# Two output projections of a two-layer decoder trunk, written as seven products of half blocks

## The chip, the core and the metric

The kernel runs on one core of one Trainium2 chip. TensorE (PE in the profile) multiplies matrices; VectorE (DVE), ScalarE (ACT) and GpSimd (POOL) work on the elements; SyncE (SP) issues nearly all the DMAs of the kernel before. Each engine works through its own list of instructions in order and waits where an operand isn't there yet. Operands lie in SBUF (128 partitions), and matmuls add into banks of PSUM. The metric is the device time of one execution in microseconds, as the median of several runs; it is smaller when the kernel is faster.

## What is computed

512 tokens of width 1024 pass through two layers and a last norm, all in float32. Each layer norms its input, projects it to many branches, makes an array of 2048 channels from them and projects that back to 1024 with a residual addition:

```python
def even_layer(x, norm_g, w_in, pool_w, pool_scale, ws, bs, w_out):
    h = rmsnorm(x, norm_g)
    z = h @ w_in
    ...
    return x + jnp.concatenate([y_a, y_b], axis=-1) @ w_out

def odd_layer(x, norm_g, w_in, conv_w, w_out):
    ...
    return x + jnp.concatenate([y_c, y_d], axis=-1) @ w_out

def reference(...):
    h = x
    for layer in range(DEPTH):      # DEPTH = 2: one even, one odd layer
        ...
    return rmsnorm(h, final_norm)
```

The change concerns the two products with `w_out` (512 x 2048 by 2048 x 1024), the additions into x behind them, and the norm that follows each.

## The kernel before

A product of two float32 arrays is made from three products of rounded parts. Each operand is split into a high part, rounded to the type of the matmul, and a low part, the rest; `mm3` adds high by high, high by low and low by high into one bank. The split of a weight tile (128 x 2048, 1 MB) is `weights`: SP loads it into `raw` (three buffers), ACT copies it to `hi` (L76), DVE subtracts to get `lo` (L77). `wh` and `wl` have two buffers each. The split of other arrays is `split` (L83 on ACT, L84 on DVE). Layer inputs are normed per tile of 128 tokens (`normed`: the addition into x on DVE, L99, squares with a sum on ACT, L100, a few tiny operations, two scalings on DVE, L110), then turned to channels on the partitions by PE and split again (`to_channels`: L119 on PE, L123 on ACT, L124 on DVE). The split layer input is `hth` and `htl`, two tiles that both layers use.

The array to be projected back is held as eight tiles `y[c]` of 256 channels by 512 tokens. The last operation on each half of them is a multiplication on Pool: L293 in the even layer (by the gate `sggb`, one operation for 256 channels), L489 and L519 in the odd layer. The Pool operation for the last tile runs while the projection has already begun.

`out_proj` does the projection in eight chunks c of 256 channels (`eo` after the even layer, `oo` after the odd one). A chunk loads and splits one weight tile (`eow`, `oow`) and splits `y[c]` (`eoy`, `ooy`); then for four token tiles t, two halves of the output h and two groups k of 128 channels it makes the three matmuls of `mm3`, 48 in a chunk and 384 in a projection, into eight banks. What ends it is a function given by the caller: `into_odd` takes chunks 6 and 7 token tile by token tile, norms each and begins to transpose tiles 0 and 1 between the matmuls; `finish` does the same for the final norm and stores the result. After the first projection the first product of the odd layer is `near` (bank and tile `v`, 96 matmuls in two groups c of two token tiles), which transposes tiles 2 and 3 before its second group; then comes `gates` (`gc`).

The order of work on each engine is the order in which the program writes it, apart from what waits for operands and for free buffers.

Of the kernel before, what the change touches and what calls it, by code (L numbers as in the profile page):

```python
# [9 lines left out]
F32 = mybir.dt.float32  # L10
# [20 lines left out]
def trunk(ctx, tc, x, w_even, w_eout, pool_w, ws_t, bs, par, g_even, w_odd, w_oout, g_odd, g_fin, cst, out):  # L31
# [19 lines left out]
    hth = cp.tile([P, KT, S], FR, name="hth")  # L51
    htl = cp.tile([P, KT, S], FR, name="htl")
    y = [cp.tile([P, 2, S], F32, name=f"y{c}") for c in range(8)]
# [8 lines left out]

    eps = cp.tile([P, 64], F32, name="eps")[:, 0:2]
# [4 lines left out]
    def weights(src, name, pieces=1):  # L68
        raw = wp.tile([P, CH], F32, tag="raw", name="r" + name, bufs=3)
# [3 lines left out]
        for i in range(pieces):  # L73
            at = slice(i * n, (i + 1) * n)
            nc.sync.dma_start(raw[:, at], src[:, at])
            A.activation(hi[:, at], raw[:, at], AF.Copy)  # L76
            V.tensor_sub(lo[:, at], raw[:, at], hi[:, at].bitcast(F32))  # L77
        return hi, lo

# [13 lines left out]
    def normed(tt, g, name, acc=None, then=None):  # L93
        o = sp.tile([P, D], F32, tag="xn", name=name, bufs=2)
# [20 lines left out]
    def to_channels(tt, o):  # L115
# [36 lines left out]
    def out_proj(src, name, last):  # L152
        acc = [[bank(f"{name}{t}{h}") for h in range(2)] for t in range(TT)]
        parts = {}

        def load(c):
            wh, wl = weights(src[c], f"{name}w{c}")
            parts[c] = (wh.rearrange("p (k d) -> p k d", k=2), wl.rearrange("p (k d) -> p k d", k=2),
                        *split(y[c], wp, "y", f"{name}y{c}"))

        def step(c, t, halves=(0, 1)):
            wh, wl, yh, yl = parts[c]
            tok = slice(t * P, (t + 1) * P)
            for h in halves:
                cols = slice(h * S, (h + 1) * S)
                for k in range(2):
                    mm3(acc[t][h], yh[:, k, tok], yl[:, k, tok], wh[:, k, cols], wl[:, k, cols],
                        c == 0 and k == 0, c == 7 and k == 1)
# [15 lines left out]
    with ExitStack() as ec:  # L184
# [6 lines left out]
        def v_half(c):  # L191
# [17 lines left out]
            if c == 0:  # L209
                load(0, 4)  # L210
                to_channels(0, normed(0, ge, "xa0"))
# [12 lines left out]
                for t in range(2):  # L224
                    step(t, 0)
                    step(t, 1)
                    to_channels(t + 1, o)
                    o = normed(t + 2, ge, f"xa{t + 2}")
                step(2, 0)
                to_channels(3, o)  # L230
# [50 lines left out]
        def mixer_b(g, vb):  # L281
# [9 lines left out]
            project(w_even[6 + 4 * g], f"u{g}", lambda j, acc: V.tensor_mul(mf[:, j, :], acc, mf[:, j, :]))  # L291
            sg = gate(w_even[7 + 4 * g], f"gb{g}")
            G.tensor_mul(mf, mf, sg)  # L293

# [9 lines left out]
    def into_odd(step, acc):  # L304
        def norm(t):
            o[t] = normed(t, go, f"xb{t}", acc[t])

        for t in range(2):
            step(6, t)
            step(7, t)  # L310
            norm(t)
        step(6, 2)
        to_channels(0, o[0])
        step(6, 3)
        step(7, 2)
        norm(2)
        to_channels(1, o[1])
        step(7, 3)
        norm(3)

    out_proj(w_eout, "eo", into_odd)
# [3 lines left out]
    with ExitStack() as oc:  # L325
# [3 lines left out]
        def values(p):  # L329
# [3 lines left out]
            def near():  # L333
# [168 lines left out]

        for c in range(4):
            dc, cv, zz = ([ap.tile([P, S + 2], F32, tag=f"qk{2 * i + j}", name=f"{n}{c}{j}", bufs=1) for j in range(2)]
# [24 lines left out]
    def finish(step, acc):  # L529
        for t in range(TT):  # L530
            for h in range(2):
                step(6, t, (h,))
                step(7, t, (h,))
# [86 lines left out]
```

## Time and profile before

| what | value |
|---|---|
| median of 3 runs | 1123.62 us (1123.47 to 1124.34) |
| the profiled execution | 1124.62 us |
| its span, first to last instruction | 1122.9 us |
| PE busy | 1105.0 us (98%) |
| DVE busy | 452.0 us (40%) |
| ACT busy | 357.5 us (32%) |
| POOL busy | 142.6 us (13%) |
| moved by DMA | 104.98 MB, mean 93 GB/s |
| first projection, first matmul to the next stage | 253.65 to 342.74 us |
| second projection, first matmul to the last addition | 1028.18 to 1115.65 us |

The profile is of one execution. Busy shares are averages over the whole span; what bounds a stretch is read from that stretch. Matmuls overlap in the records: the distance between two of them is the time that one costs, not the duration in its row.

### The profile page before, as it was taken

The page shows a single profiled execution, that of the slowest core. Times are in us where ns is not written, and L with a number is a line of the kernel's source. Part 1 is how long each engine was busy: PE and PEld are TensorE (multiplying, and loading weights), DVE is VectorE, ACT ScalarE, POOL GpSimd, SP SyncE. Part 2 cuts the span into 40 slices and gives each one's busy share as a digit, 9 for nine tenths or more (in the row PEclk, how much of TensorE's full clock was granted, in tenths as well). Part 3 has the DMA queues.
Part 4 walks back from the last instruction along what each step waited for, and adds up shares of the span by engine and source line. Part 5 has one row for each costly group of instructions (what it writes and reads, how often), then busy time and mean ns, then how long its engine had stood idle before and what let it go on. Part 6 is the DMA issues. An engine that isn't in the chain of part 4 may idle for free.

```text
span 1122.9 us, 12809 instructions
## 1 busy us (share of the span) xinstructions
PE 1105.0 (98%) x5288; PEld 945.4 (84%) x5288; DVE 452.0 (40%) x617; ACT 357.5 (32%) x532; POOL 142.6 (13%) x460
## 2 busy tenths in 40 slices
PE   6999999999999999999999999999999999999997
PEld 5888888888888988899889988899888888888885
DVE  6344315343256225433345225442445442432326
ACT  5323223222235224432424224332424222121323
POOL 0001000101000004320224004220124011011000
PEclk9999999999999999999999999999999999999999
DMA  9232232322323231222221221322221222323211
GB/s 331 88 118 85 75 112 85 109 79 75 113 75 111 96 113 45 106 75 75 100 90 62 89 93 57 105 84 76 81 108 44 107 90 99 113 76 113 76 38 75
DMA packets 18282, 104.98 MB, mean 93 GB/s; under 512 B 2096, under 2 KB 3248, under 8 KB 6704
## 3 DMA queue, kind: packets, MB, share of 16 engines
q1 hardware_dynamic: 18224, 104.17, 26.5%
q8 instruction: 41, 0.67, 0.2%
q14 instruction: 17, 0.14, 0.0%
HBM read 102.06 MB, written 2.10 MB: 93 GB/s over the span
## 4 chain that ended last, share of the span: by engine, by line
PE 98%; DMA 1%; ACT 0%; DVE 0%; SPq 0%; issue 0%; DVEq 0%
PE q L90 8%; PE q L88 8%; PE q L89 8%; PE v L88 6%; PE v L90 5%; PE v L89 5%; PE oo L88 3%; PE eo L90 3%; PE eo L88 3%; PE oo L90 3%; PE eo L89 3%; PE oo L89 3%; PE gc L88 1%; PE gc L89 1%; PE gc L90 1%; PE dx L90 1%
## 5 line engine op out<-in xcount | busy, mean ns | idle before, releaser
L88 PE MATMUL q<-hth,hq 128*128 128x512 f32 x384 | 150.5, 392 | 0.0
L90 PE MATMUL q<-hth,lq 128*128 128x512 f32 x384 | 149.6, 389 | 0.0
L89 PE MATMUL q<-htl,hq 128*128 128x512 f32 x384 | 149.5, 389 | 0.0
L88 PE MATMUL v<-hv,hth 128*128 128x512 f32 (+1 forms) x320 | 114.8, 359 | 0.9 <-ACT hth L123 0.9
L90 PE MATMUL v<-hv,htl 128*128 128x512 f32 (+1 forms) x320 | 112.8, 353 | 0.0
L89 PE MATMUL v<-lv,hth 128*128 128x512 f32 (+1 forms) x320 | 112.6, 352 | 0.0
L90 PEld LDWEIGHTS q<-hth,lq 128*128 128x128 f32 x384 | 72.1, 188 | 15.1
L89 PEld LDWEIGHTS q<-htl,hq 128*128 128x128 f32 x384 | 72.1, 188 | 14.6
L88 PEld LDWEIGHTS q<-hth,hq 128*128 128x128 f32 x384 | 72.2, 188 | 14.4
L88 PEld LDWEIGHTS v<-hv,hth 128*128 128x128 f32 x320 | 76.6, 239 | 4.7 <-ACT hth L123 2.1
L90 PEld LDWEIGHTS v<-hv,htl 128*128 128x128 f32 x320 | 76.5, 239 | 3.2 <-DVE htl L124 0.7
L89 PEld LDWEIGHTS v<-lv,hth 128*128 128x128 f32 x320 | 76.8, 240 | 2.7
L77 DVE TENSOR_TENSOR lq<-rq,hq 128x2048 fp32r<-128x2048 f32 x24 | 54.9, 2289 | 51.2 <-ACT hq L76 51.2
L76 ACT ACTIVATE hq<-rq 128x2048 fp32r<-128x2048 f32 x24 | 46.0, 1915 | 76.5 <-PE q L89 55.4
L77 DVE TENSOR_TENSOR lv<-rv,hv 128x2048 fp32r<-128x2048 f32 (+1 forms) x22 | 37.4, 1704 | 39.2 <-ACT hv L76 39.2
L90 PE MATMUL eo<-heow,leoy 128*128 128x512 f32 x128 | 49.9, 390 | 0.0
L89 PE MATMUL eo<-leow,heoy 128*128 128x512 f32 x128 | 49.8, 389 | 0.0
L88 PE MATMUL eo<-heow,heoy 128*128 128x512 f32 x128 | 49.8, 392 | 0.0
L89 PE MATMUL oo<-loow,hooy 128*128 128x512 f32 x128 | 49.7, 389 | 0.0
L90 PE MATMUL oo<-hoow,looy 128*128 128x512 f32 x128 | 49.7, 389 | 0.0
L88 PE MATMUL oo<-hoow,hooy 128*128 128x512 f32 x128 | 49.5, 390 | 0.0
L76 ACT ACTIVATE hv<-rv 128x2048 fp32r<-128x2048 f32 (+1 forms) x22 | 31.6, 1446 | 55.8 <-PE v L90 17.0
(218 smaller groups left out, 2167.7 us busy)
## 6 DMA issues: line engine op xcount, KB each, us to landing
rq<-in_w_odd SPq DMA_DIRECT2D x24, 1024.0 KB, 4.7
rv<-in_w_odd SPq DMA_DIRECT2D x12, 1024.0 KB, 4.7
reow<-in_w_eout SPq DMA_DIRECT2D x8, 1024.0 KB, 4.8
roow<-in_w_oout SPq DMA_DIRECT2D x8, 1024.0 KB, 4.7
ra<-in_w_even SPq DMA_DIRECT2D x4, 1024.0 KB, 4.7
rga<-in_w_even SPq DMA_DIRECT2D x4, 1024.0 KB, 5.5
ru<-in_w_even SPq DMA_DIRECT2D x4, 1024.0 KB, 4.8
rgb<-in_w_even SPq DMA_DIRECT2D x4, 1024.0 KB, 4.7
```

What stands on the lines that cost most here:

```text
L76: A.activation(hi[:, at], raw[:, at], AF.Copy)
L77: V.tensor_sub(lo[:, at], raw[:, at], hi[:, at].bitcast(F32))
L88: T.matmul(acc, ah, bh, start=first, stop=False)
L89: T.matmul(acc, ah, bl, start=False, stop=False)
L90: T.matmul(acc, al, bh, start=False, stop=last)
```

## The change

Both projections are done in Strassen's form. y is cut into 2 x 2 blocks (1024 channels by 256 tokens, `block[i, h]`, in one tile `yy`), w_out into four blocks of 1024 by 512, each stored as two tiles q of 1 MB. Seven products of half size replace the eight block products. Each product has two weight tiles q, two token tiles t and four groups k: 48 matmuls. They come in the order 1 (bank X), 7 (Z), 5 (Y), 2 (X), 6 (Y), 4 (Z), 3 (Y).

- **Sums of y** are made in place on DVE, each 128 x 2048 elements: b00-=b01 before the projection (`prepare`), b01-=b11, b00+=b11, b10-=b00 in it. `form` then makes the high part on ACT and the low part on DVE, into one tile of a ring of three buffers, which `hth` and `htl` share.
- **Sums of weights** are made by DMAs of GpSimd's queue that add a block to a tile that SP has loaded: r7 = block 1 + block 3; r5 = block 0 + block 1, later += block 3 (product 6) and += block 2 (product 4). Products 1, 2 and 3 use blocks as they are. A projection has 10 loads of 1 MB by SP and 8 adding DMAs of 1 MB. The two r5 tiles have a pool of their own, whose memory belonged to the layer's own pool until then.
- **Additions into x**: what is shared by several outputs is copied once, the first by ACT (s1), the second by a DVE subtraction (v), and Pool adds or subtracts these in x, two and four operations of 128 x 512; DVE adds the rest from the banks.
- **Order at the seams**: tiles 2 and 3 are normed before and in the last product, tiles 0 and 1 in its second half and behind it; tile 2 is turned to channels in its middle, tile 3 right behind it, and `near` does its second group first, with the transposes of tiles 0 and 1 ahead of the other. `xn` has three buffers.

```diff
-        for c in range(6):
-            load(c)
-            for t in range(TT):
-                step(c, t)
-        load(6)
-        load(7)
-        last(step, acc)
+    def ring(name):
+        return cp.tile([P, KT * S], FR, tag="act", name=name, bufs=3)
...
+        def form(self, view, n):
+            f = ring(f"{self.name}f{n}").rearrange("p (w k t) -> p w k t", w=2, k=KT)
+            A.activation(f[:, 0], view, AF.Copy)
+            V.tensor_sub(f[:, 1], view, f[:, 0].bitcast(F32))
+            return f
+
+        def load(self, n, q, blocks, pool=None):
+            name = f"r{self.name}{n}{q}"
+            raw = pool.tile([P, CH], F32, tag=name, name=name) if pool else raw_tile(name)
+            nc.sync.dma_start(raw, self.src[blocks[0], q])
+            for b in blocks[1:]:
+                G.dma_start(raw, self.src[b, q], accum_op=ALU.add)
+            return raw
+
+        def add(self, raw, b, q):
+            G.dma_start(raw, self.src[b, q], accum_op=ALU.add)
...
+        def product(self, z, first, f, w, q, t, last=False):
...
+            for k in range(4):
+                kk = 4 * q + k
+                go, end = first and kk == 0, last and kk == KT - 1
+                T.matmul(acc, f[:, 0, kk, tok], wh[:, k, :], start=go, stop=False, skip_group_check=True)
+                T.matmul(acc, f[:, 0, kk, tok], wl[:, k, :], start=False, stop=False, skip_group_check=True)
+                T.matmul(acc, f[:, 1, kk, tok], wh[:, k, :], start=False, stop=end, skip_group_check=True)
...
+        def prepare(self):
+            b = self.block
+            self.f1 = self.form(b[0, 0], 1)
+            V.tensor_sub(b[0, 0], b[0, 0], b[0, 1])
...
+            w1 = [self.parts(self.load(1, q, [0]), 1, q) for q in range(2)]
+            f7 = self.form(b[0, 0], 7)
+            r7 = [self.load(7, q, [1, 3]) for q in range(2)]
...
+            V.tensor_sub(b[0, 1], b[0, 1], b[1, 1])
+            both("X", True, self.f1, w1)
+            w7 = [self.parts(r7[q], 7, q) for q in range(2)]
+            s1 = sp.tile([P, 2, S], F32, tag="xn", name=f"{nm}s1", bufs=3)
+            for t in range(2):
+                A.activation(s1[:, t, :], acc["X", t], AF.Copy)
+            r5 = [self.load(5, q, [0, 1], pool) for q in range(2)]
+            f5 = self.form(b[0, 1], 5)
+            both("Z", True, f7, w7)
+            V.tensor_add(b[0, 0], b[0, 0], b[1, 1])
+            w5 = [self.parts(r5[q], 5, q) for q in range(2)]
+            for t in range(2):
+                G.tensor_sub(x(t, 1), x(t, 1), s1[:, t, :])
+                V.tensor_sub(x(2 + t, 1), x(2 + t, 1), acc["Z", t])
+            f2 = self.form(b[1, 0], 2)
+            both("Y", True, f5, w5)
+            w2 = [self.parts(self.load(2, q, [2]), 2, q) for q in range(2)]
+            for q in range(2):
+                self.add(r5[q], 3, q)
...
+            both("X", False, f2, w2, True)
+            V.tensor_sub(b[1, 0], b[1, 0], b[0, 0])
+            w6 = [self.parts(r5[q], 6, q) for q in range(2)]
+            for q in range(2):
+                self.add(r5[q], 2, q)
...
+            both("Y", False, f6, w6)
+            w4 = [self.parts(r5[q], 4, q) for q in range(2)]
+            v = sp.tile([P, 2, S], F32, tag="xn", name=f"{nm}v", bufs=3)
+            for t in range(2):
+                V.tensor_sub(v[:, t, :], acc["Y", t], s1[:, t, :])
+                G.tensor_add(x(2 + t, 1), x(2 + t, 1), v[:, t, :])
+                G.tensor_sub(x(2 + t, 0), x(2 + t, 0), v[:, t, :])
+            f3 = self.form(b[1, 0], 3)
+            both("Z", False, f4, w4, True)
+            w3 = [self.parts(self.load(3, q, [3]), 3, q) for q in range(2)]
+            for t in range(2):
+                V.tensor_add(x(2 + t, 0), acc["Z", t], x(2 + t, 0))
+                half1(t)
+            for t in range(2):
+                for q in range(2):
+                    self.product("Y", False, f3, w3, q, t, True)
+                V.tensor_add(x(t, 1), acc["Y", t], x(t, 1))
+                half0(t)
...
-                for c in range(2):
+                for c in (1, 0):
                     acc = bank(f"v0{p}{c}")
                     for i in range(2):
-                        if p == 0 and c:
-                            to_channels(2 + i, o[2 + i])
+                        if p == 0 and not c:
+                            to_channels(i, o[i], hth, htl)
```

DVE's list at the beginning of the first projection, before. `leow` is the low part of a chunk's weights, `leoy` that of its y, the figure behind it the chunk:

```order
L77 TENSOR_TENSOR leow0_1609<-reow0_1607,heow0_1608 128x2048
L276 SCALAR_TENSOR_TENSOR y3_77<-mx31_1528,pr_69,sgga3_1391 128x512
L77 TENSOR_TENSOR leow1_1667<-reow1_1665,heow1_1666 128x2048
L84 TENSOR_TENSOR leoy2_1730<-y2_76,heoy2_1729 128x1024
L77 TENSOR_TENSOR leow2_1725<-reow2_1723,heow2_1724 128x2048
```

The same place now. `leo70` is the low part of product 7's weights of half q = 0, `eof7` the form of y for product 7, `yy<-yy` a sum in place (L209 b00-=b01, L229 b01-=b11, L238 b00+=b11):

```order
L175 TENSOR_TENSOR eof1_1529<-yy_72,eof1_1529 128x2048
L209 TENSOR_TENSOR yy_72<-yy_72 128x8x256
L87 TENSOR_TENSOR leo11_1608<-reo11_1605,heo11_1607 128x2048
L229 TENSOR_TENSOR yy_72<-yy_72 128x8x256
L175 TENSOR_TENSOR eof7_1611<-yy_72,eof7_1611 128x2048
L87 TENSOR_TENSOR leo70_1672<-reo70_1614,heo70_1671 128x2048
L175 TENSOR_TENSOR eof5_1688<-yy_72,eof5_1688 128x2048
L238 TENSOR_TENSOR yy_72<-yy_72 128x8x256
L87 TENSOR_TENSOR leo71_1676<-reo71_1617,heo71_1675 128x2048
L175 TENSOR_TENSOR eof2_1754<-yy_72,eof2_1754 128x2048
L87 TENSOR_TENSOR leo50_1743<-reo50_1682,heo50_1742 128x2048
```

Where a weight tile's low part came every 48 matmuls with one smaller split beside it, two come now, with a form and a sum between them; the sum of L229 reads the part of y that Pool's last multiplication writes, and stands ahead of product 7's weights.

Pool's list around the same place, before: the even layer's four multiplications, then the odd layer's preparation for attention.

```order
L293 TENSOR_TENSOR y_80<-y_80,sggb_1249 128x1024
L293 TENSOR_TENSOR y_81<-y_81,sggb_1536 128x1024
L400 TENSOR_SCALAR bias_2648<-cs 128x256
L400 TENSOR_SCALAR bias_2648<-cs 128x128 x2
```

Pool's list now. `reo` are raw weight tiles (1614 and 1617 for product 7, 1682 and 1685 are r5), `eos` is s1, `eov` is v:

```order
L395 TENSOR_TENSOR yy<-yy,sggb_1242 128x1024
L183 DMA reo_1614<-in_w_eout 128x2048
L183 DMA reo_1617<-in_w_eout 128x2048
L395 TENSOR_TENSOR yy<-yy,sggb_1533 128x1024
L183 DMA reo_1682<-in_w_eout 128x2048
L241 TENSOR_TENSOR xt<-xt,eos_1679 128x512
L183 DMA reo_1685<-in_w_eout 128x2048
L241 TENSOR_TENSOR xt<-xt,eos_1679 128x512
L187 DMA reo_1682<-in_w_eout 128x2048
L187 DMA reo_1685<-in_w_eout 128x2048
L187 DMA reo_1682<-in_w_eout 128x2048
L187 DMA reo_1685<-in_w_eout 128x2048
```

The adding DMAs and the Pool operations on x share one queue, in this order; the DMAs for product 7 stand ahead of the last multiplication, those for product 5 behind it.

## Rows read from the trace of the kernel before

**Rows 1.** The page: span, busy time, granted clock, chain that ended last.

```profile
span 1122.9 us, 12809 instructions
...
PE 1105.0 (98%) x5288; PEld 945.4 (84%) x5288; DVE 452.0 (40%) x617; ACT 357.5 (32%) x532; POOL 142.6 (13%) x460
...
PEclk9999999999999999999999999999999999999999
...
PE 98%; DMA 1%; ACT 0%; DVE 0%; SPq 0%; issue 0%; DVEq 0%
```

**Rows 2.** The page's groups: projection matmuls; busy us, mean ns of one, idle before.

```profile
L88 PE MATMUL eo<-heow,heoy 128*128 128x512 f32 x128 | 49.8, 392 | 0.0
...
L88 PE MATMUL oo<-hoow,hooy 128*128 128x512 f32 x128 | 49.5, 390 | 0.0
```

**Rows 3.** ACT over time in the first projection: start us, us, operation, [idle before].

```profile
275.38 1.06 ACT L83 ACTIVATE heoy<-y 128x1024 fp32r<-128x1024 f32 x1 [8.01 <-PE eo L89]
...
286.26 1.06 ACT L83 ACTIVATE heoy<-y 128x1024 fp32r<-128x1024 f32 x1 [8.01 <-PE eo L89]
```

**Rows 4.** Groups by line and shape, DVE: busy us, mean ns of one.

```profile
L77 DVE TENSOR_TENSOR leow<-reow,heow 128x2048 fp32r<-128x2048 f32 x8 | 18.3, 2291 | 13.7 <-ACT heow L76 13.7
...
L110 DVE SCALAR_TENSOR_TENSOR xb<-xt,stxb,go 128x512 f32<-128x512 f32 x8 | 5.7, 750 | 0.1
...
L99 DVE TENSOR_TENSOR xt<-eo,xt 128x512 f32<-128x512 f32 x8 | 5.5, 687 | 3.9 <-PE eo L90 3.8
```

**Rows 5.** Groups by line and shape, ACT.

```profile
L76 ACT ACTIVATE heow<-reow 128x2048 fp32r<-128x2048 f32 x8 | 15.2, 1905 | 13.9 <-issue 9.2 <-PE gb L89 4.6
```

**Rows 6.** All engines over time at the start of the first projection.

```profile
253.65 0.39 PE L88 MATMUL eo<-heow,heoy 128*128 128x512 f32 x1
...
255.62 2.29 DVE L77 TENSOR_TENSOR leow<-reow,heow 128x2048 fp32r<-128x2048 f32 x1 [10.40 <-ACT heow L76]
...
256.14 4.02 POOL L293 TENSOR_TENSOR y<-y,sggb 128x1024 f32<-128x1024 f32 x1 [44.08 <-ACT sggb L245]
```

**Rows 7.** All engines over time at the start of the second projection.

```profile
1028.18 0.39 PE L88 MATMUL oo<-hoow,hooy 128*128 128x512 f32 x1
...
1030.10 2.29 DVE L77 TENSOR_TENSOR loow<-roow,hoow 128x2048 fp32r<-128x2048 f32 x1 [8.58 <-ACT hoow L76]
...
1030.62 2.91 POOL L519 TENSOR_TENSOR y<-cv,dc 128x512 f32<-128x512 f32 x1 [5.71 <-ACT dc L518]
```

**Rows 8.** Pool's operations on y: least, median and greatest ns.

```profile
L489 POOL TENSOR_TENSOR y<-y,yo x8: 1286/1290/1294, 461.4 to 883.8; 128x512 f32<-128x512 f32 x8
L519 POOL TENSOR_TENSOR y<-cv,dc x8: 1306/2108/2912, 893.1 to 1030.6; 128x512 f32<-128x512 f32 x8
```

**Rows 9.** The page's DMA issues: KB each, median us to landing.

```profile
roow<-in_w_oout SPq DMA_DIRECT2D x8, 1024.0 KB, 4.7
```

**Rows 10.** Stretches: us, busy of each engine, PEclk, DMA share, GB/s.

```profile
core 0: us, PE busy (x) PEld busy (x) DVE busy (x) ACT busy (x) POOL busy (x), PEclk, DMA share, GB/s
12.00:15.00 3.00, 3.00 (x9) 2.28 (x8) 2.54 (x7) 3.00 (x9) 0.00 (x0) 1.00 1.05 412
253.65:342.74 89.09, 89.09 (x402) 73.60 (x400) 36.50 (x40) 29.80 (x34) 4.99 (x4) 1.00 0.25 85
342.74:357.31 14.57, 14.13 (x115) 13.48 (x113) 9.81 (x21) 6.36 (x12) 0.00 (x0) 1.00 0.45 171
```

**Rows 11.** DMA issues in the first 40 us: KB each, median us to landing.

```profile
ru<-in_w_even SPq DMA_DIRECT2D x1, 1024.0 KB, 10.2
```

**Rows 12.** The end of the kernel over time.

```profile
1115.22 0.39 PE L90 MATMUL oo<-hoow,looy 128*128 128x512 f32 x1
...
1118.30 1.42 DVE L110 SCALAR_TENSOR_TENSOR xc<-xt,stxc,gf 128x512 f32<-128x512 f32 x2
```

More of the change, by code (lines that the diff above doesn't have):

```diff
@@ L50, in trunk @@
     bsb = cp.tile([P, 4, P], F32, name="bsb")
-    hth = cp.tile([P, KT, S], FR, name="hth")
-    htl = cp.tile([P, KT, S], FR, name="htl")
-    y = [cp.tile([P, 2, S], F32, name=f"y{c}") for c in range(8)]
+    yy = cp.tile([P, 2 * KT, S], F32, name="yy")
+    y = [yy[:, 2 * c:2 * c + 2, :] for c in range(8)]
     ident = cs[:, 0:128]
@@ L61, in gain, with activations @@
         return t
+    def ring(name):
+        return cp.tile([P, KT * S], FR, tag="act", name=name, bufs=3)
+    def activations(name):
+        return tuple(ring(f"{name}{i}").rearrange("p (k t) -> p k t", k=KT) for i in "hl")
+    hth, htl = activations("he")
     eps = cp.tile([P, 64], F32, name="eps")[:, 0:2]
@@ L65, in trunk, with raw_tile, parts_of @@
     A.activation(eps[:, 1:2], eps[:, 0:1], AF.Sqrt)
-    def weights(src, name, pieces=1):
-        raw = wp.tile([P, CH], F32, tag="raw", name="r" + name, bufs=3)
+    def raw_tile(name):
+        return wp.tile([P, CH], F32, tag="raw", name=name, bufs=3)
+    def parts_of(raw, name, pieces=1, src=None):
         hi = wp.tile([P, CH], FR, tag="wh", name="h" + name, bufs=2)
@@ L74, in weights @@
             at = slice(i * n, (i + 1) * n)
-            nc.sync.dma_start(raw[:, at], src[:, at])
+            if src is not None:
+                nc.sync.dma_start(raw[:, at], src[:, at])
             A.activation(hi[:, at], raw[:, at], AF.Copy)
@@ L78, in weights @@
         return hi, lo
+    def weights(src, name, pieces=1):
+        return parts_of(raw_tile("r" + name), name, pieces, src)
     def split(raw, pool, tag, name, bufs=2, lo_eng=None):
@@ L93, in normed @@
     def normed(tt, g, name, acc=None, then=None):
[L94 removed]
+        o = sp.tile([P, D], F32, tag="xn", name=name, bufs=3)
         st = sp.tile([P, 64], F32, tag="st", name="st" + name, bufs=4)
@@ L302, in trunk, with norm1, norm0 @@
     o = {}
[L304 to L321, printed above, removed]
+    odd = []
+    def norm1(t):
+        o[2 + t] = normed(2 + t, go, f"xb{2 + t}")
+    def norm0(t):
+        if not odd:
+            odd.extend(activations("ho"))
+        to_channels(2 + t, o[2 + t], *odd)
+        o[t] = normed(t, go, f"xb{t}")
+    even_out.run(norm1, norm0)
+    hth, htl = odd
     slopes = [2.0 ** (-8.0 * (n + 1) / (SLOTS * N_DIL)) for n in range(SLOTS * N_DIL)]
@@ L527, in trunk, with finish @@
     gf = gain(g_fin, "gf")
[L529 to L533, printed above, removed]
-            normed(t, gf, f"xc{t}", acc[t],
-                   lambda h, v: nc.sync.dma_start(out[t * P:(t + 1) * P, h * S:(h + 1) * S], v))
-    out_proj(w_oout, "oo", finish)
+    def finish(t):
+        normed(t, gf, f"xc{t}", then=lambda h, v: nc.sync.dma_start(out[t * P:(t + 1) * P, h * S:(h + 1) * S], v))
+    odd_out.run(lambda t: finish(2 + t), finish)
 def _constants():
@@ L582, in _layout, with blocks @@
     w_odd = np.concatenate(parts)
-    def rows(w):
-        return np.ascontiguousarray(np.asarray(w)[0].reshape(8, 2, P, D).transpose(0, 2, 1, 3)).reshape(8, P, CH)
+    def blocks(w):
+        return np.asarray(w)[0].reshape(2, 2, 4, P, 2, S).transpose(0, 4, 1, 3, 2, 5).reshape(4, 2, P, CH)
     par = np.concatenate([np.asarray(i["even_pool_scale"])[0].reshape(8, P), np.asarray(i["odd_conv_w"])[0].reshape(24, P)])
@@ L590, in _layout @@
         "w_even": w_even,
-        "w_eout": rows(i["even_w_out"]),
+        "w_eout": blocks(i["even_w_out"]),
         "pool_w": np.asarray(i["even_pool_w"])[0].reshape(4, 2, P, 256).transpose(0, 2, 1, 3).reshape(4, P, 512),
@@ L597, in _layout @@
         "w_odd": w_odd,
-        "w_oout": rows(i["odd_w_out"]),
+        "w_oout": blocks(i["odd_w_out"]),
         "g_odd": np.asarray(i["odd_norm"])[0],
```

57 lines of the change are left out of this document (39 added, 18 removed).

## The prediction, made before the changed kernel was run

> **What bounds the kernel now.** I read the page first. PE is busy for 1105.0 of 1122.9 us, the chain that ended last is 98% PE, and the granted clock stays in the top tenth throughout, so a matmul taken away in the two projections takes its time off the end, as long as nothing else becomes late [rows 1]. Next the matmul groups: each projection has 3 x 128 of them, 384 [rows 2]. ACT's list over time gives the beat: the splits of y for two neighbouring chunks begin at 275.38 and 286.26, so a chunk of 48 matmuls takes 10.88 us, 0.2267 us each [rows 3] (a "mean of one" near 390 ns is a pipelined duration, not a beat). The stretches show that the first projection leaves DVE busy for 36.5 of 89.1 us, ACT 29.8 and the DMA engines a quarter [rows 10]. There is room on average; whether it lies where it is needed is the question. Below, t is the time since a projection's first matmul, and hnq, lnq are the high and the low part of product n's weights of half q (heo71 is h71).
>
> **What is removed.** Seven products of 48 matmuls replace eight chunks of 48: 336 for 384, with the same shapes. 2 x 48 x 0.2267 = **-21.8 us**. This term is certain.
>
> **What is added, on average.** Every product needs two weight tiles split (before: one), each 1.91 us on ACT and 2.29 on DVE [rows 4, 5], one form of y (a DVE subtraction of the same 2048 elements, 2.29) and, in four of seven cases, a sum of y in place (again 2048 elements from SBUF, 2.29). With two additions into x of 0.69 [rows 4] a product puts 4 x 2.29 + 2 x 0.69 = 10.5 us on DVE, against 10.88 on PE. So DVE has no slack left at the beginning of the row, and every operation that is late there reaches PE. ACT has three copies of 1.9 and is not the limit.
>
> **A: product 7's low weights.** In DVE's order l70 (leo70) follows l11, the sum b01-=b11 and f7's low part. That sum reads the last part of y, which Pool multiplies: 256.14 + 4.02 = 260.16, t = 6.5 [rows 6]; in the second projection 1030.62 + 2.91, t = 5.35 [rows 7]. Three operations of 2.29 behind it end at 6.5 + 6.87 + 0.2 (three hand-overs) = 13.6; the first low-weight matmul is due at 10.88 + 0.23 = 11.1: **+2.5**, and with 5.35 **+1.3**. Before, nothing on DVE waited for that multiplication except chunk 7's split, some 76 us later.
>
> **B: its second half.** l71 stands behind f5 low and b00+=b11: 13.6 + 3 x 2.29 = 20.5; due 24 matmuls after 13.6, at 19.0: **+1.4**, in both projections +2.8.
>
> **C: product 5 and the adding DMAs.** r50 and r51 lie in memory that the layer's last gate used, so their plain loads stand on SP behind Pool's multiplication: 6.5 + 4.7 for 1 MB [rows 9] = 11.2. Then GpSimd's queue adds the second block. The trace has no adding DMA and none from GpSimd. The nearest rows: a plain 1 MB load lands in 4.7, and one queued among others at the start in 10.2 [rows 9, 11]. At 412 GB/s [rows 10] 1 MB streams in 2.55 us, so 4.7 is 2.15 fixed and 2.55 of stream. An adding transfer has to fetch what stands in the tile as well as the source; I take two streams, 2.15 + 5.1 = 7.25, near the middle of 4.7 and 10.2. Beside it run the plain loads of r51 and r20 (2.55 each): 11.5 + 7.25 + 5.1 = 23.9. Copy and subtraction end at 23.9 + 1.9 + 2.3 = 28.1. Product 7 ends at 10.88 + 2.5 + 1.4 + 10.88 = 25.7, so the low weights, due at 25.9, are 2.2 late, and with hand-overs 2.4. r51: all that the queues must move from 11.2 on is 3 x 2.55 + 2 x 5.1 = 17.85, plus 2.15: 31.2; split at 35.5; due at 28.2 + 5.4 = 33.5: 2.0. Sum 4.4, taken as **4.5** in each projection, +9.0. If the sums land in 4.7 nothing of it remains; at 9.8 it is 9.3 each.
> "Collectives: The Full Stack" of the Trainium skill (the bandwidth ceiling) says of a reducing transfer that the addition costs nothing but needs two source reads, so that the rate halves; no run of before shows it. By it the price would be the 7.25 that I take. "DMA: Bandwidth & Descriptors" of the Trainium skill (Anatomy of one DMA) gives 2.0 us + bytes/436e3 for one from GpSimd, an estimate of 4.4 us for 1 MB of plain copy, and by that alone C would be nothing.
>
> **D: product 4.** Its sum goes out when product 6's half is split, about 0.7 us before product 6 starts: there at 6.5 after that start, split at 10.8: just in time, but l40 then holds DVE while the bank of token tile 0, complete since 8.2, waits for its subtraction. That ends at 11.5, Pool's addition into x at 12.8 (1.29, [rows 8]), ACT's square for the norm at 13.6, and only behind this square stands h41: 15.5, l41 at 18.1 with hand-overs; due 10.88 + 5.44 + 0.23 = 16.6: **+1.5** each, +3.0. With early sums 0.4 each.
>
> **The seam to the odd layer.** Before, the 14.57 us from the last projection matmul to the second kind of work held 96 v matmuls at 0.12, two tiles of transposes and about 1.0 us of waiting [rows 10]. Now tiles 2, 3 come first; the low part of the v weights stands on DVE behind scalings of 1.42 (two of 0.75, [rows 4]) and lowers of the transposes, 2.2 late, and tiles 0 and 1 wait for the norm that can begin only after the last product, 2.0 more: 4.2 against 1.0, **+3.2**.
>
> **The tail.** Before, 4.3 us pass from the last matmul's end (1115.45) to the end of the last scaling (1118.30 + 1.42) [rows 12]. In the last product DVE now has the scalings of three tiles; that of tile 0 (1.42) stands ahead of the last addition: **+1.5**.
>
> **Sum.** -21.8 + 3.8 (A) + 2.8 (B) + 9.0 (C) + 3.0 (D) + 3.2 + 1.5 = +1.5. The profiled run took 1124.62 (span 1122.9 and 1.7 around it); that is 1.0 above the median of the runs, 1123.62. So 1126.1 for a run like the profiled one, and 1123.62 + 1.5 = **1125.1** as the median. Costless, since covered: the extra copies on ACT; the 10 more loads and sums per projection in bandwidth (now a quarter of the DMA engines, [rows 10]); the longer DVE time in later products, where DVE has 10 us or less per 10.88.
>
> **Rivals.**
> 1. *The sums hide* (faster). If an adding DMA lands in about 4.7, C is 0 and D 0.8: -21.8 + 3.8 + 2.8 + 0.8 + 3.2 + 1.5 = -9.7, **1114**. For it: plain transfers stream at 412 GB/s and the engines are idle for three quarters. Against: each sum needs more traffic than a load.
> 2. *DVE also waits for Pool.* L519 takes 1.31 us or, beside a DVE subtraction from SBUF, 2.91, and L293 ends 2.25 after such a subtraction [rows 6 to 8]: Pool waits for DVE. Whether DVE waits for Pool as well no row shows. If so, Pool's two x subtractions (1.29 each) in product 7 push l71 by 2.6 and the four of product 4 push l41 by 1.0, 3.6 per projection. When product 5 waits for sums anyway, 2.6 of it goes unseen: 1125.1 + 2.1 = **1127**; with hidden sums 1114 + 7.2 = **1121**.
> "SBUF — State Buffer" of the Trainium skill (Who interferes with whom) says that the pair of ports shared by DVE and GpSimd is an exclusive lock and that the one issued second fully blocks, a DVE instruction with two SBUF inputs against GpSimd's reads among them; the trace agrees for Pool waiting (2.91 for 1.31), and by the rule this rival would hold.
> 3. *Slow sums* (slower). Eight 1 MB sums per projection follow each other through one queue, six of them on the same two tiles, each later one ready to go only once the earlier value is split. From about 7 us of landing time each more microsecond lands on PE. At three streams (9.8, near the 10.2 of [rows 11]) r50 comes at 28.6, C is 9.3 and D 4.4: 7.7 more per projection, **1141**; at 2.15 + 10.2 PE waits in every product with sums, some 1168. For it: the chain load, sum, split, sum is serial, and none of its links has a row. Against: nothing in the trace moves at less than half of 412 GB/s when it streams.
> That the change does less than it says is small: the matmul count is fixed by the order.
>
> **How the numbers follow.** Forecast 0.33, spread 1119 to 1132 by landing times of 6.3 to 8.2 us. Rival 1 0.28, 1111 to 1117. Rival 2 0.17, 1119 to 1130. Rival 3 0.22, 1134 and more. Within 0.2% (2.25 us, about what a measurement of this kernel can tell from no change) lies 1121.4 to 1125.9. Faster: 0.08 + 0.28 + 0.03 = 0.39. Same: 0.11 + 0.06 = 0.17. Slower: 0.14 + 0.08 + 0.22 = 0.44. As both signs hold much, the forecast's own range is 1119 to 1132; the range for 8 in 10 is 1111 to 1147, leaving out the end of rival 3 and a little below rival 1.
>
> **What the new profile would show.** PE matmuls 96 fewer and the beat unchanged; gaps of PE with the releaser "DVE leo" at t = 10.9 (2.5 and 1.3) and near 19 (1.4), at product 5 and once in product 4. The adding DMAs' landing time in the list of issues decides between forecast and rivals 1 and 3: 7 to 8, under 5, over 9. A DVE subtraction of 2.29 that grows beside Pool's 1.29 shows rival 2. Wrong would be: PE gaps in products 2, 6 or 3, a lower granted clock after gaps, or a multiplication by Pool that ends later than 6.5 and moves A.

## The result

The changed kernel takes 1130.08 us (median of 5 runs, 1130.01 to 1134.71), the kernel before 1123.47 on the same chip: 6.6 us more, ratio 1.0066 (95% interval 1.0047 to 1.0086). The forecast was 1125.1, its own range 1119 to 1132.

The page of the changed kernel: span, busy time, granted clock over the span, and the chain that ended last.

```profile
span 1128.4 us, 12730 instructions
...
PE 1092.4 (97%) x5192; PEld 930.2 (82%) x5192; DVE 518.6 (46%) x643; ACT 391.2 (35%) x546; POOL 178.8 (16%) x488
...
PEclk9999999999999999999999999999999999999899
...
PE 84%; DMA 7%; issue 3%; DVE 3%; ACT 2%; POOL 1%; SPq 0%; DVEq 0%; ACTq 0%; POOLq 0%
```

Set against [rows 1]: PE has 96 matmuls fewer, yet is busy only 12.6 us less, and the chain, once 98% PE, now runs through DMA, DVE and ACT for 12% of the span. The clock's row shows an 8 where there was none.

Stage by stage, worked out from the first and the last projection matmul of both traces (us, each figure rounded by itself; a matmul's beat of 0.23 added to the last):

| | to the first `eo` matmul | first projection | to the first `oo` matmul | second projection | to the end of the span | span |
|---|---|---|---|---|---|---|
| before | 253.7 | 89.1 | 685.4 | 87.3 | 7.5 | 1122.9 |
| changed | 253.3 | 90.4 | 687.7 | 89.2 | 7.9 | 1128.4 |

336 matmuls at 0.2267 are 76.2. With one tile of transposes (0.9) in the first projection, 13.3 us are lost in it, and 13.0 in the second. Where, PE's list of waits tells (engine and line, what it waited for: us in total, times, longest us):

```profile
PE ooZ L202 <- DVE loo L87: 6.3, 4, 2.8
PE eoZ L202 <- DVE leo L87: 5.5, 4, 2.1
PE eoY L202 <- DVE leo L87: 2.5, 2, 1.4
PE ooY L202 <- DVE loo L87: 1.8, 1, 1.8
```

11 waits, 16.2 us, all for the low part of a weight tile: product 7 and 4 (bank Z), product 5 (bank Y), the places of terms A to D. The rest is mostly a slower PE behind such waits. PE over time at the first one (start us, us, operation, [idle before]): a matmul starts every 0.23 us ahead of the wait and every 0.42 behind it.

```profile
263.95 0.39 PE L203 MATMUL eoX<-heo,eof 128*128 128x512 f32 x1
264.17 0.39 PE L201 MATMUL eoZ<-heo,eof 128*128 128x512 f32 x1
266.60 0.63 PE L202 MATMUL eoZ<-leo,eof 128*128 128x512 f32 x1 [2.04 <-DVE leo L87]
267.02 0.63 PE L203 MATMUL eoZ<-heo,eof 128*128 128x512 f32 x1
```

The granted clock (PEclk) of stretches of the changed kernel:

```profile
core 0: us, PE busy (x) PEld busy (x) DVE busy (x) ACT busy (x) POOL busy (x), PEclk, DMA share, GB/s
262.00:264.17 2.17, 2.17 (x11) 1.79 (x10) 2.17 (x2) 2.00 (x2) 0.00 (x0) 1.00 1.04 438
266.60:270.00 3.40, 3.40 (x8) 2.66 (x9) 3.40 (x2) 2.06 (x2) 3.40 (x3) 0.53 1.04 316
...
324.72:328.20 3.48, 3.48 (x8) 2.73 (x9) 2.15 (x1) 0.00 (x0) 2.94 (x3) 0.52 0.21 40
1052.29:1055.30 3.01, 3.01 (x7) 2.43 (x8) 2.15 (x1) 0.00 (x0) 0.00 (x0) 0.50 1.08 231
1062.50:1065.50 3.00, 3.00 (x8) 2.34 (x7) 1.32 (x1) 1.55 (x1) 0.00 (x0) 0.50 0.97 161
...
253.29:343.66 90.37, 82.30 (x345) 65.61 (x344) 65.11 (x51) 46.27 (x43) 21.15 (x16) 0.96 0.68 183
1031.36:1120.53 89.17, 81.04 (x337) 64.55 (x335) 65.00 (x53) 43.98 (x40) 18.91 (x14) 0.96 0.64 165
```

Four stretches of 3.0 to 3.5 us run at 1.2 GHz instead of 2.4, behind waits of 2.04, 2.12, 2.83 and 1.83 us. At the clocks of these rows about 6.3 of their 12.9 us would not have been needed. (The fifth long wait, 2.10 at 1104.09, is followed by none.)

So the sum as measured, over the span: -21.8 for the matmuls, +16.2 of waits, +6.3 of clock, about +3.3 in the restarts behind the waits and other small gaps, +1.4 at the seam (2.3 longer, of which 0.9 is a tile of transposes that stood inside the projection before), +0.4 at the end, -0.4 at the start: +5.4, against 5.5 between the two spans.

### The profile page after: what moved, and what is told of

Its sections match the earlier page's. It is cut to its first block, busy times and chain, and to the rows that moved or that the text cites. A ratio compares the mean times of both kernels' runs of the same rounds, so it can differ in the third digit from the quotient of the medians.

```text
span 1128.4 us, 12730 instructions
## 1 busy us (share of the span) xinstructions
PE 1092.4 (97%) x5192; PEld 930.2 (82%) x5192; DVE 518.6 (46%) x643; ACT 391.2 (35%) x546; POOL 178.8 (16%) x488
## 4 chain that ended last, share of the span: by engine, by line
PE 84%; DMA 7%; issue 3%; DVE 3%; ACT 2%; POOL 1%; SPq 0%; DVEq 0%; ACTq 0%; POOLq 0%
PE q L102 8%; PE q L101 8%; PE q L103 8%; PE v L101 6%; PE v L102 5%; PE v L103 5%; DMA roo<-in_w_oout 3%; DMA reo<-in_w_eout 3%; PE gc L101 1%; PE gc L103 1%; PE gc L102 1%; PE dc L103 1%; PE dc L102 1%; PE dx L103 1%; PE u L101 1%
## 5 line engine op out<-in xcount | busy, mean ns | idle before, releaser
L101 PE MATMUL q<-hoh,hq 128*128 128x512 f32 x384 | 150.5, 392 | 0.0
L103 PE MATMUL q<-hoh,lq 128*128 128x512 f32 x384 | 149.6, 389 | 0.0
L102 PE MATMUL q<-hol,hq 128*128 128x512 f32 x384 | 149.5, 389 | 0.0
L101 PE MATMUL v<-hv,hoh 128*128 128x256 f32 (+1 forms) x256 | 88.5, 346 | 0.3 <-ACT hoh L136 0.3
L102 PE MATMUL v<-lv,hoh 128*128 128x256 f32 (+1 forms) x256 | 87.2, 341 | 1.2 <-DVE lv L87 1.2
L103 PE MATMUL v<-hv,hol 128*128 128x256 f32 (+1 forms) x256 | 87.1, 340 | 0.0
L103 PEld LDWEIGHTS q<-hoh,lq 128*128 128x128 f32 x384 | 72.1, 188 | 15.1
L101 PEld LDWEIGHTS q<-hoh,hq 128*128 128x128 f32 x384 | 72.1, 188 | 14.6
L102 PEld LDWEIGHTS q<-hol,hq 128*128 128x128 f32 x384 | 72.1, 188 | 14.5
L102 PEld LDWEIGHTS v<-lv,hoh 128*128 128x128 f32 x256 | 64.3, 251 | 1.5 <-DVE lv L87 1.4
L86 ACT ACTIVATE heo<-reo 128x2048 fp32r<-128x2048 f32 x14 | 26.8, 1914 | 44.7 <-DMA reo<-in_w_eout 12.3
```

Of the source, the lines that this page charges most:

```text
L101: T.matmul(acc, ah, bh, start=first, stop=False)
L102: T.matmul(acc, ah, bl, start=False, stop=False)
L103: T.matmul(acc, al, bh, start=False, stop=last)
```

## The experiments

All times are medians; "to before" is the difference to the kernel before on the same chip in the same hour (its median there between 1123.8 and 1124.3). The changed kernel stands at +6.6.

**What the saved matmuls are worth: e6.** The kernel before, one chunk less per projection.

```diff
-        for c in range(6):
+        for c in range(5):
             load(c)
```

> The kernel before with one of the eight chunks of each projection left out (chunk 5: its load, its splits and its 48 matmuls). What 96 matmuls fewer are worth with nothing added: 2 x 10.88 less than before, 1101.7 to 1102.6. If PE's beat weren't what ends the projections, it would be less.

1102.72, -21.1 to before. 96 matmuls are worth what their beat says, less 0.7.

**What the sums of weights cost: e1 and e9.** e1 has no adding DMAs; e9 has them as plain copies on the same queue.

```diff
-                G.dma_start(raw, self.src[b, q], accum_op=ALU.add)
+                G.dma_start(raw, self.src[b, q])
```

> The changed kernel without its 16 adding DMAs: each tile of weights that should be a sum stays at its first block, and everything else is as it is. My theory: the adding DMAs land in 8.0 us and product 5 waits for them, 1.1 + 1.4 us of PE in the first projection and 1.8 in the second, with one stretch at the lower clock behind the last (1.7), and product 4 in part (0.5 of 2.6). Without them 1130.1 - 6 to 8 = 1122 to 1124, the waits of product 7 and of product 4's second half unchanged. Rival (the sums are hidden, only DVE's order bounds): within 1.5 us of 1130.

> The changed kernel with its 16 DMAs of GpSimd's queue as plain copies, without the addition (the weights of products 7, 5, 6 and 4 are then the last block, not sums). Theory (an adding transfer moves two streams): landing falls from 8.0 to about 5.5 us, 2.55 less, product 5 waits 3 to 5 us less per projection where it still waits, 1120 to 1126. Rival (it is the queue of GpSimd that is slow): about 8 us as before, and 1130.

e1: 1117.86, -6.1 to before (ratio 0.9944, 0.9928 to 0.9961), so 12.7 better than the changed kernel; more than expected. e9: 1118.47, -5.8 (0.9948, 0.9928 to 0.9968), also below its expectation. In both, product 5 waits no more, product 4 waits 1.1 instead of 2.3 and 2.6, and the granted clock of the projections is 0.98 for 0.96. My expectation of e1 held the waits that went (7 us) and one stretch at the lower clock; two of the four went, and small gaps with them. The issues by DMA (KB each, median us to landing), the changed kernel:

```profile
reo<-in_w_eout SPq DMA_DIRECT2D x10, 1024.0 KB, 5.7
...
reo<-in_w_eout POOLq DMA_DIRECT2D x8, 1024.0 KB, 8.0
```

and e9:

```profile
reo<-in_w_eout SPq DMA_DIRECT2D x10, 1024.0 KB, 4.8
...
reo<-in_w_eout POOLq DMA_DIRECT2D x8, 1024.0 KB, 5.2
```

The addition alone makes 8.0 of 5.2: 2.8 us more, where one more stream at [rows 10]'s 412 GB/s is 2.55. These medians are those of transfers with little beside them. The two sums that product 5 waits for run beside plain loads and take longer; r50's and r51's in the first projection of the changed kernel:

```profile
reo<-in_w_eout POOLq DMA_DIRECT2D x1, 1024.0 KB, 12.3
...
reo<-in_w_eout POOLq DMA_DIRECT2D x1, 1024.0 KB, 17.1
```

and of e9:

```profile
reo<-in_w_eout POOLq DMA_DIRECT2D x1, 1024.0 KB, 9.4
...
reo<-in_w_eout POOLq DMA_DIRECT2D x1, 1024.0 KB, 10.1
```

There the addition makes 2.9 and 7.0 us. Without it, and nothing else changed, the kernel is 12.4 us better and faster than before. By a straight line between the two medians, an estimate, the change would be worth nothing at 8.0 - 2.8 x 6.6/12.4 = 6.5 us of landing; the prediction's spread (1119 at 6.3, 1132 at 8.2) puts that point at 7.0.

The Trainium skill's "Collectives: The Full Stack" (the bandwidth ceiling) gives a reducing transfer half the rate, since it reads two sources; the runs agree for the stream (2.55 for one read; with the 2.8 on top about 5.3, an estimate) and not for the whole time (8.0 for 5.2). The Trainium skill's "DMA: Bandwidth & Descriptors" (Anatomy of one DMA) would give 4.4 us, an estimate, for the plain copy; measured 5.2, and for the adding one 8.0.

**Whether the waits add up: e2 and e12.** e2 keeps the sums and moves only what DVE does: b01-=b11 behind product 7's first low weights, the second ahead of f5's low part. e12 does that and leaves the sums out.

```diff
-            V.tensor_sub(b[0, 1], b[0, 1], b[1, 1])
...
             w7 = [self.parts(r7[q], 7, q) for q in range(2)]
+            s01 = V.tensor_sub(b[0, 1], b[0, 1], b[1, 1])
+            later(s01, lows[f"{nm}70"])
...
             f5 = self.form(b[0, 1], 5)
+            later(lows[f"{nm}f5"], lows[f"{nm}71"])
```

> The changed kernel with another order on DVE alone: the sum b01-=b11 goes behind product 7's first low weights, and product 7's second low weights ahead of f5's low part, so that what waits for Pool's last multiplication no longer stands before them. Theory: the waits of product 7 go (2.0 + 1.2 and 0.9 + 2.8 us) with their two or three stretches at the lower clock (about 3.5), 10 in all; but the tiles r50 and r51 hang on the same multiplication (their loads reuse the gate's memory), land when they did, and product 5 now waits for them by nearly as much as product 7 had waited: 1127 to 1131. Rival (each wait stands by itself): 1119 to 1121.

> Both of these together: no adding DMAs, and the new order on DVE (the weights of products 7, 5, 6 and 4 aren't sums). Theory: with the sums gone nothing takes back what DVE's order gives: the waits of products 7 and 5 (12 us) go with four stretches at the lower clock (6 to 7), and product 4's square remains: 1110 to 1114. Rival (each stands by itself): the gains of the two single runs added.

e2: 1131.42, +7.4 to before, nothing gained. e12: 1115.42, -8.6 (0.9929, 0.9914 to 0.9943), 2.4 better than e1. So one wait takes the place of another as long as the sums come late: in e2's second projection product 5 waits 4.8 + 1.5 us, where the changed kernel waited 2.8 for product 7 and 1.8 for product 5. But e12 lies between its expectation and its rival (1.4 above the one; the gains added would give some 1119), and neither run removed all that it was to remove: product 7's first low weights are still 2.05 us late in e2's first projection, and 3.14 in e12's. DVE in e2:

```profile
255.13 2.29 DVE L89 TENSOR_TENSOR leo<-reo,heo 128x2048 fp32r<-128x2048 f32 x1 [3.80 <-ACT heo L88]
257.41 4.41 DVE L181 TENSOR_TENSOR eof<-yy,eof 128x2048 fp32r<-128x2048 f32 x1
261.93 2.29 DVE L246 TENSOR_TENSOR yy<-yy 128x2048 f32<-128x2048 f32 x1
```

and Pool in e2:

```profile
255.66 4.02 POOL L403 TENSOR_TENSOR yy<-yy,sggb 128x1024 f32<-128x1024 f32 x1 [5.16 <-ACT sggb L353]
```

f7's low part, which needs nothing from Pool, takes 4.41 instead of 2.29 while Pool multiplies. Before, Pool waited for DVE there [rows 6]; here DVE waits for Pool.

**Whether DVE waits for Pool: e3.** Pool's two subtractions of s1 in product 7 are left out.

```diff
-                G.tensor_sub(x(t, 1), x(t, 1), s1[:, t, :])
```

> The changed kernel without Pool's two subtractions of s1 in x per projection, in product 7. Theory (DVE waits for Pool): the DVE operations of 2.29 us that take 3.4 beside them go back to 2.29, so product 7's second low weights come 2.2 us earlier and the wait for them falls from 1.2 to 0 and from 2.8 to 0.6 us; product 5's wait for r50 grows in exchange, so the time moves by less than 2 us, 1128 to 1130. Rival (DMA traffic or descriptor writing makes them long): 3.4 us stay.

One run, 1130.15. DVE in product 7, the changed kernel (f5's low part, b00+=b11):

```profile
264.26 2.29 DVE L87 TENSOR_TENSOR leo<-reo,heo 128x2048 fp32r<-128x2048 f32 x1
266.46 3.38 DVE L175 TENSOR_TENSOR eof<-yy,eof 128x2048 fp32r<-128x2048 f32 x1
269.76 3.37 DVE L238 TENSOR_TENSOR yy<-yy 128x2048 f32<-128x2048 f32 x1
```

and e3:

```profile
266.40 2.28 DVE L175 TENSOR_TENSOR eof<-yy,eof 128x2048 fp32r<-128x2048 f32 x1
268.61 2.28 DVE L238 TENSOR_TENSOR yy<-yy 128x2048 f32<-128x2048 f32 x1
```

The 1.1 us of each are gone, with the same DMA traffic beside them (295 GB/s from 266.4 to 273.0 in both). Product 7's second wait fell from 1.2 to 0 and from 2.8 to 0.6; product 5's grew by 1.7 in the first projection and 1.9 in the second, and the time stayed. "SBUF — State Buffer" of the Trainium skill (Who interferes with whom) says that either of the two can be the one that is blocked, by which issued second; the trace agrees in both directions, Pool's 2.91 for 1.31 before [rows 7, 8] and DVE's 3.38 for 2.28 here.

**Whether the clock falls for the gaps: e4.** 32 matmuls per projection into a bank that nobody reads, where PE waits.

```diff
+                if k == 0 and fill:
+                    spare = bank(f"{self.name}fill{z}{q}{first}")
+                    for i in range(fill):
+                        T.matmul(spare, f[:, 0, kk, tok], wh[:, k, :], start=i == 0, stop=i == fill - 1)
...
-            both("Z", True, f7, w7)
+            both("Z", True, f7, w7, fill=(8, 6))
```

> The changed kernel with extra matmuls into a bank that nobody reads, placed where PE waits: 8 and 6 ahead of product 7's two low weights, 5 and 5 in product 5, 8 in product 4's second half, 0.227 us each, from operands that are there. Theory: the granted clock falls because PE stands idle for about 2 us, and four such falls cost 7 us; with the gaps filled the clock stays at its higher level in both projections. What is gained in product 7 (3.5) comes back as waiting in product 5, what is gained behind it (3.5) stays, less up to 1.5 where a filler outlasts its wait: 1126 to 1129. Rival (the fall has another reason than the gap): the beats of 0.43 us behind the waits stay, and the time is 1130 to 1133.

1128.86, +4.9 to before (1.0044, 1.0029 to 1.0059; the changed kernel's interval overlaps it). The two projections of e4:

```profile
252.60:341.80 89.20, 86.52 (x377) 69.24 (x377) 65.46 (x52) 46.22 (x43) 21.14 (x16) 1.00 0.70 186
1029.20:1117.80 88.60, 85.53 (x369) 68.27 (x367) 64.99 (x53) 43.73 (x40) 18.86 (x14) 1.00 0.65 166
```

With the gaps filled the granted clock is 1.00 through both, where it is 0.96 in the changed kernel: it falls because PE stands idle. That the time hardly moves is no contradiction: the fillers cost 7.3 us per projection, 2.6 and 3.1 us of waits remain beside them, and product 5 waits for the same transfers whenever PE comes.

Not every such gap has its fall, though. In e2 PE waits 2.05 us for the same l70, until 266.48, and the matmuls behind it run at the full clock (columns as above):

```profile
266.48:269.90 3.42, 3.42 (x15) 2.85 (x16) 3.42 (x2) 0.29 (x2) 3.42 (x3) 1.00 1.06 311
```

So the cost differs from run to run of one kernel as well: e2's five go from 1126.39 us, at a mean granted clock of 0.996, to 1134.35 at 0.989, and 0.007 of the span is 7.9 us of the 8.0 between them. What decides whether a gap of 2 us has a fall stays open here.

**Another order of the products: e5 and e7.** Products 1, 7, 2, 5, 6, 3, 4, so that product 5 starts at 32.6 us, when r50 and r51 are there; e7 is the same without the adding DMAs.

```diff
-            both("Z", True, f7, w7)
-            both("Y", True, f5, w5)
-            both("X", False, f2, w2, True)
-            both("Y", False, f6, w6)
-            both("Z", False, f4, w4, True)
+            both("Z", True, f7, w7)
+            both("X", False, f2, w2, True)
+            both("Y", True, f5, w5)
+            both("Y", False, f6, w6, True)
+            both("W", True, f3, w3, True)
```

> The same computation in another order: products 1, 7, 2, 5, 6, 3, 4 instead of 1, 7, 5, 2, 6, 4, 3, product 3 with banks of its own; on DVE the low weights ahead of the sums of y; Pool's subtraction of s1 gone, since v is added to both; tiles 0 and 1 normed first, 2 and 3 at the end. Product 5 then starts at about 32.6 us, after r50 (24) and r51 (31) have landed, and product 4 comes a product later than its sums. Theory: waits of at most 2 us per projection and no stretch at the lower clock; of the 13 us per projection that the changed kernel loses 11 to 12 come back: 1105 to 1109. Rival (the chain of sums is too slow in any order, or the matmuls saved are not worth their 10.9 us): 1115 and more, with PE waiting in products 6 and 4.

> The other order without the adding DMAs (the weights of products 7, 5, 6 and 4 aren't sums). Theory: in this order the sums are hidden but for the late half of product 6 or 4: 0 to 3 us faster than with them. Rival: if the chain of sums still bounds, 6 us or more faster.

e5: 1128.79, +5.0 to before: 20 us above what I expected, and the rival's mark. e7: 1120.40, -3.4, so 8.4 better than e5, its rival's mark too: in this order the chain of sums still bounds. Product 5 indeed waits for nothing, but product 6 now stands right behind it and needs the same tiles with another block added. ACT's copy of product 6's first half (h60) in e5, and PE at product 6's start:

```profile
295.50 1.92 ACT L88 ACTIVATE heo<-reo 128x2048 fp32r<-128x2048 f32 x1 [6.46 <-DMA reo<-in_w_eout]
```

```profile
302.69 0.50 PE L207 MATMUL eoY<-heo,eof 128*128 128x512 f32 x1 [4.77 <-DVE xt L265]
```

The sum was issued at 286.18 and there at 295.50; copy and subtraction end at 299.7; behind them on DVE stand f3's low part and x += Y, which must read the bank before product 6 writes it: 4.8 us of waiting. In e7, without sums, 1.8 us of it are left, so 3.0 are the sum's. Load, split, sum, split of one tile takes more than one product. That was written in the prediction as a link without a row; I forgot it when I made e5.

**The uses of one tile 16 us apart: e8.** Product 3, whose weights are no sum, is cut in halves that go between: 1, 7, 2, 5, half of 3, 6, the other half, 4; x += Y ahead of product 6's low weights; the squares of the norm behind product 4's high weights.

```diff
-            both("Y", False, f6, w6, True)
-            both("W", True, f3, w3, True)
+            for t in range(2):
+                self.product("W", True, f3, w3, 0, t)
...
+            for t in range(2):
+                self.product("Y", False, f6, w6, 0, t)
...
+            for t in range(2):
+                self.product("Y", False, f6, w6, 1, t, True)
...
+            for t in range(2):
+                self.product("W", False, f3, w3, 1, t, True)
...
+            for t in range(2):
+                self.product("Z", False, f4, w4, 0, t)
```

> The order of the run before, mended where it waited: product 6 came right behind product 5 although r5 + block 3 needs 8 to 9 us of transfer and 4.2 of splitting between them, and the squares of the norm stood ahead of product 4's high weights. Now product 3 (plain weights) is cut in halves and spread: 1, 7, 2, 5, first half of 3, 6, second half of 3, 4, so that 16 us lie between two uses of the same tile; ACT's copy of f2 comes behind product 7's first high weights, x += Y ahead of product 6's low weights, the squares behind product 4's. Theory: every sum fits (r6 about 2 to 4 us and r4 about 3 us ahead of their splits), DVE has no operation in a row that PE waits for; PE waits at most 1 to 2 us in each projection and the clock stays up: of 26 us lost 22 to 24 come back, 1106 to 1109. Rival (the traffic and the work themselves are too much, in any order): 1115 or more, with waits spread over the products.

1113.32, -11.0 to before (0.9907, 0.9890 to 0.9923): faster than both kernels, with the same computation. The two projections of e8:

```profile
252.70:334.00 81.30, 78.25 (x345) 63.47 (x344) 64.81 (x49) 46.38 (x42) 21.86 (x16) 1.00 0.74 205
1023.60:1101.40 77.80, 77.08 (x337) 62.64 (x335) 61.11 (x45) 42.15 (x35) 20.21 (x14) 1.00 0.70 177
```

The second needs 77.8 us for matmuls that take 76.2. The adding DMAs land no sooner (10.6 us, median of six, in the first projection); what grew is the distance between two uses of a tile. The expectation (1106 to 1109) is missed by what lies outside: to the first `oo` matmul it takes 689.6 (before: 685.4), to the end of the span 9.9 (before: 7.5).

**The norms at the ends, and one square: e10 and e11.** e10 changes e8's ends; e11 is e10 with the square of tile 2's finished half behind product 4's second high weights, as e8 had it.

```diff
-            if behind is not None and h:
+            if behind is not None and (h or late):
                 later(sq, behind)
```

> The spread order with its ends mended: of the squares of the norms only the last half of each tile stays behind product 4's high weights, tiles 2 and 3 square their finished half first, and DVE makes the odd layer's first low weights ahead of the scalings of tile 1. In the spread order the two projections had become 17 us shorter (-7.8 and -9.4), but the seam to the odd layer 4.1 us longer than in the kernel before and the tail some 2.5. Theory (these are waits of the norms' chain): 2 to 4 us of the 6.6 come back, 1109 to 1111. Rival (the last product by weight halves instead of by token tiles costs them, in any order of the squares): within 1 us of 1113.3.

> The run before with one operation of ACT per projection moved: the square of tile 2's finished half, which waits for Pool's addition into x, goes behind product 4's second high weights instead of ahead of them. In the run before the ends had become shorter (the seam by 2.4 us, the tail by 1.4), but product 4 waited 2.7 us twice (0.9 for the high, 1.8 for the low weights), at the same place where the changed kernel waits. Theory (term D: one square in ACT's row that waits for Pool costs product 4 2.7 us): the 5.5 us go and the shorter ends stay, 1110 to 1113. Rival (the wait has another reason): 1117 to 1119.

e10: 1118.67, -5.6 to before, slower than e8 and outside both its expectation and its rival; e11: 1114.16, -10.1 (0.9915, 0.9902 to 0.9929), 1.2 above its expectation and not to be told from e8. e10's ends did become shorter (687.0 and 8.5), but product 4 waits 0.9 + 1.8 us in each projection. ACT in e10, the square and then h41:

```profile
325.48 0.63 ACT L119 ACTIVATE xb<-xt 128x512 f32<-128x512 f32 x1 [6.65 <-POOL xt L287]
326.02 0.19 ACT L119 ACTIVATION_READ_ACCUMULATOR xb<-xt 128x1 f32 x1
326.11 1.90 ACT L92 ACTIVATE heo<-reo 128x2048 fp32r<-128x2048 f32 x1
```

and h41 in e11:

```profile
321.41 1.92 ACT L92 ACTIVATE heo<-reo 128x2048 fp32r<-128x2048 f32 x1 [2.96 <-PE eoW L211]
```

One operation of 0.6 us that waits for Pool, ahead of a weight split in ACT's row, makes the two projections 6.7 us longer (166.6 for 159.9 in the profiled executions, one stretch at the lower clock included); the medians differ by 4.5. What e11 gave back at the end (10.9 for 8.5) I did not look into; a version with e8's middle and e10's ends was not run.

## Why the prediction came out as it did

- **The matmuls**: -21.8, measured -21.1 (e6). Right.
- **A**: forecast 2.5 and 1.3, measured 2.04 and 0.88. Right in place and mechanism; the subtraction that waits for Pool's multiplication stands where the order had it. The 0.2 for hand-overs had no row, and there are none: DVE's operations of 2.29 start 2.20 apart.
- **B**: forecast 1.4 each, measured 1.21 and 2.83. Both are mis-sized: in each projection two DVE operations up to l71 took 3.4 instead of 2.29 beside Pool's subtractions of s1, 2.2 us in all. This is rival 2, which I gave 0.17 and which e3 shows to hold. That the first came out near 1.4 is luck: the slow matmuls ahead of it took 1.6 us of the lateness.
- **C**: forecast 4.5 each, measured 1.12 + 1.42 and 1.83. The arrival of the sums was right: I had r50 at t = 23.9 and r51 at 31.2, and they landed at 24.3 and 31.5 (ACT's copy of r50 below); the lone landing time of 7.25 was 8.0. But PE came to product 5 later than forecast, in the first projection at 27.2 instead of 25.7, held up by the clock, in the second by B as well, and every microsecond lost there was one less here. e2 shows the same from the other side.

```profile
277.72 1.92 ACT L86 ACTIVATE heo<-reo 128x2048 fp32r<-128x2048 f32 x1 [9.06 <-DMA reo<-in_w_eout]
```

- **D**: forecast 1.5 each, measured 0.16 + 2.12 and 0.50 + 2.10. The mechanism is in part the one named, a square that waits for Pool and stands ahead of h41, in the changed kernel's ACT list:

```profile
318.80 0.63 ACT L113 ACTIVATE xb<-xt 128x512 f32<-128x512 f32 x1 [4.33 <-POOL xt L264]
...
319.43 1.90 ACT L86 ACTIVATE heo<-reo 128x2048 fp32r<-128x2048 f32 x1
```

  In the spread order e10 and e11 show it by moving that one operation. The other part is rival 2 again: l41 itself took 3.31 instead of 2.29 beside the last of Pool's four operations on x, in both projections, the 1.0 that the rival named; e1 and e9, with early sums, still wait 1.1 us there.

```profile
321.36 3.31 DVE L87 TENSOR_TENSOR leo<-reo,heo 128x2048 fp32r<-128x2048 f32 x1 [3.38 <-ACT heo L86]
...
321.24 1.28 POOL L265 TENSOR_TENSOR xt<-xt,eov 128x512 f32<-128x512 f32 x1
```

- **The waits together**: 18.6 forecast for A to D, 16.2 measured.
- **The clock**: forecast 0, measured about 6.3. This is the step that failed: the sum priced a wait at its length, while behind four of the five waits of some 2 us the matmuls ran at half the clock for another 3 us, 1.5 us more each time. The prediction named a lower clock after gaps only among what would make it wrong, without a price, though the trace of before has matmuls 0.43 us apart too, at its start, behind PE's first 9.6 us of waiting (where [rows 10] prints a clock of 1.00 all the same). With 6.3 more the sum would have given 1131.4.
- **Seam and tail**: forecast +3.2 and +1.5, measured +1.4 and +0.4. Both too dear: the v weights' low part was 1.2 late, not 2.2, and waits that I added one to another lay beside each other.
- **Rivals**: rival 1 did not come true, since the adding DMA lands in 8.0; e9 shows that at 5.2 it would have (-5.8 to before; rival 1 said about -9). Rival 2 did, inside the forecast: it holds in product 7 and in product 4. Rival 3 did not, at 8.0; its 28.6 for r50 does not follow from its own terms (11.5 + 9.8 + 5.1 = 26.4), and its 1168 has no working.

That 1130 lies so near the forecast owes something to errors that cancel: 6.3 us of clock and some 3 of restarts too little, 2.4 of waits and 2.9 of ends too much. The forecast's spread, read at the measured 8.0 us of landing, even gives 1130.6; that is luck, since it has C larger than it was and no clock.

## What to carry to other kernels

A wait of PE can cost more than its length, since the matmuls behind it may run slowly: here a gap of 2 us cost another 1.5 or nothing, so price it as a range. Where several waits in a row hang on one late event (here Pool's last multiplication, through DVE's row and through the memory of the tiles), removing the first moves its time to the next; the experiment that counts removes all of them, or puts the dependent work a product later, which here turned +0.66% into -0.93%. When a tile is loaded, split, added to and split again, lay out the length of that chain (here 8 us of transfer alone, 12 to 17 with other loads beside it, and 4.2 of splitting) against the distance between its two uses before choosing the order.

## What the runs showed of the hardware

- An adding DMA of 1 MB from GpSimd's queue landed in 8.0 us, a plain one from the same queue in 5.2, one from SP in 4.7 to 4.8 (medians). Beside denser traffic the adding ones took longer: 10.6 (median of six) in e8's first projection, 12.3 and 17.1 for the two of product 5 in the changed kernel's.
- DVE subtractions with both inputs in SBUF and Pool operations that read SBUF hold each other up in both directions: 2.91 for Pool's 1.31 before; 3.38 for DVE's 2.28 in the changed kernel, and 4.41 in e2.
- In the changed kernel the granted clock fell to half for 3.0 to 3.5 us behind four of five waits of 1.8 to 2.8 us, in one case 1.0 us after the wait's end (1061.08, 1062.12), and stayed at 1.00 where matmuls filled the same gaps (e4). Behind an equal wait in e2 it stayed up as well.
